# A folded Fourier projection: row-tile folds every third tile in a fixed order on two engines, and query swaps ahead of their sums

## The chip, the cores and the metric

One core of a Trainium2 chip runs the whole program in one launch. The engines are called as the profile calls them: PE (matrix multiply; PEld is its weight load), DVE (vector), ACT (scalar and activations), POOL (GpSimd), and SP, which only issues DMAs here. The metric is the device time of one execution in microseconds (us), less being better. Inputs and outputs are float32 and lie in device memory.

## The reference

Two layers of an encoder over 256 tokens and 16 learned tokens put in front (272 positions, width 2048). Cut to what matters here:

```python
h = rmsnorm(x, norm_mix[i])
proj = h @ w_in[i]                       # q | k | v | f | two gates
q, k, v = heads of proj                  # 8 query heads, 2 key/value heads, 128 wide
q = rope_2d(rmsnorm(q, q_norm[i])); k = rope_2d(rmsnorm(k, k_norm[i]))
attn = softmax(q k^T / sqrt(128)) v      # bidirectional
f = proj[..., OFF_F:OFF_GA]              # 8 groups of 128 channels
fr = fft2(f over (positions, channels of a group), norm="ortho").real
merged = sigmoid(ga) * (attn @ w_attn_br[i]) + sigmoid(gf) * (fr @ w_four[i])
x = x + merged @ w_out[i]
h2 = rmsnorm(x, norm_ffn[i])
x = x + (silu(dwconv3(h2 @ w_up_gate)) * (h2 @ w_up_val)) @ w_down[i]
```

After the second layer the 16 learned positions are dropped, so that layer computes queries and everything behind them for 258 columns, the 256 tokens and two neighbours for the convolution, while keys, values and the Fourier branch still see all 272.

## The kernel before

Activations lie transposed in on-chip memory: channels across the 128 partitions, positions along the free axis. Weights are read once, as a stream of chunks of 512 KB (128 partitions x 1024 float32; 512 contraction rows by 256 output columns). Each chunk passes through the same steps:

- SP issues its load into one of four `raw` buffers (line 179).
- ACT rounds it to the format that PE multiplies at full rate, giving the hi part `wh` (line 213); DVE subtracts that from the raw chunk, giving the lo part `wl` (line 214). Each has three buffers. The text calls these the hi split and the lo split. The lo split is the last reader of `raw`, so it releases that buffer for a later load.
- PE multiplies. A float32 product is made of three: hi weight by hi activation, hi weight by lo activation, lo weight by hi activation (lines 270, 271, 272 in `group`).

`advance(upto)` issues loads and puts splits on a list `todo`, two chunks ahead of the one that PE is at (`LOOK = 2`); `pump` takes the next split from the list, or all up to a chunk.

Besides the stream there are shadow generators: pieces of work (statistics of keys and queries, rotations, attention, folds) written as Python generators. `push(gen, wait)` adds one. After every second column product, `group` calls `step`, which counts each generator's wait down and runs the first one that is due up to its next `yield n`; n is the number of steps until it is due again. `until(hold, flag)` runs generators at once until a flag is set. So the yields set where in the written program the pieces of side work lie.

A scheduler then orders each engine's instructions from the written program and its own estimates. Within `tc.manual_schedule(engines={...})` the named engines keep the written order. Each engine executes its instructions strictly in order, and waits at an instruction until its inputs and buffers are ready.

The second layer (`last`, `lo = 14`) goes k, v, q0, q1, then the folded projection `f4`, then q2, q3 and the gates. A real 2-D transform over positions is even or odd under reflection, so the normalized activations are folded: for each row tile of 128 channels the sum and the difference of position t and its mirror position, 138 columns each, are multiplied with folded weights. The pieces, all of the second layer:

- `fold_pair(b)` (before) makes the folded row tiles 2b and 2b + 1. DVE multiplies by the norm (`t1`, line 645), adds (`hf`, 647); ACT copies two unpaired columns (648); DVE subtracts (649). Then, for each tile, ACT scales and rounds to the hi part (654), and DVE makes the lo part from it (655). There are eight slots, five in `hA` and three in `hB`.
- `fold_ahead` is a shadow generator that makes tiles 0 to 7 during earlier groups, from v on. `folded_f` makes tiles 8 to 15 while PE works on tiles 0 to 7, whose slots they take over.
- `folded_f` (line 663 on) runs over k = 0 to 15. One tile of work on PE is one weight chunk: four groups of channels by two halves, in eight banks, each with a hi product of hi and lo activations in one matmul (line 682) and a lo product (686). One pair of small matmuls for a separate column lies behind the first hi product of each tile (685). At k = 15 the groups are finished in the order 2, 3, 0, 1, and `E` is evacuated: ACT copies (689), DVE adds (690), ACT copies `e64` (692). Groups 2 and 3 lie in the same rotating set of banks ("mm") as the results of q0, q1, q2, so tile 0 needs q1's banks free, and q2 needs those of groups 2 and 3 free.
- `warm` (line 695) is a tiny Exp that loads ACT's table.
- `head_evac` takes a q or k group from its banks: per bank ACT squares (750) and DVE scales (751).
- `q_stage` and `kstats` are the generators behind q and k: `sums_t` transposes squares on PE (758) and reduces them on DVE (759); POOL raises to the power -1/2 (`pow_half`, 409); `swap` moves partition quarters by four DMAs (764) for the rotation; `rope` multiplies by sine and cosine (768 and 769), adds (770), rounds to hi on ACT (771), subtracts to lo on DVE (772). For keys, DVE spreads the factors along a mask (`dk`, 801), PE multiplies by ones to broadcast them (`ps_kb`, 804), and DVE applies them (805).

In this part of the kernel DVE keeps the written order from q1's evacuation through `folded_f`; ACT is ordered by the scheduler.

Of the kernel before, what the change touches and what calls it, by code (L numbers as in the profile page):

```python
# [20 lines left out]
T = NM + SEQ  # L21
# [107 lines left out]
def encoder_kernel(ctx, tc, xT, params, consts, bmat, cfold, csign, w_fl, w_f64c, w_in, w_abr, w_four, w_f64, w_out, w_up, w_down, outT):  # L129
# [77 lines left out]

    def split_w(i, a, b):
        if i not in splits:
            splits[i] = tuple(wp.tile([P, CW, MG * P], F32R, tag=t, name=f"{t}{i}") for t in ("wh", "wl"))  # L210
        h, lo = splits[i]
        r = raws[i]
        nc.scalar.copy(h[:, a:b], r[:, a:b])  # L213
        nc.vector.tensor_tensor(lo[:, a:b], r[:, a:b], h[:, a:b].bitcast(F32), op=ALU.subtract)  # L214
        if b == CW:
            del raws[i]

    shadow = []

    def push(gen, wait=0):  # L220
        shadow.append([wait, gen])
# [254 lines left out]
    for l in range(DEPTH):  # L476
# [6 lines left out]
        with tc.tile_pool(name=f"mix{l}", bufs=1) as mp:  # L483
# [158 lines left out]

            def fold_pair(b, slots):
                t1 = rt("t1")
                nc.vector.tensor_tensor(t1, XT[:, 2 * b:2 * b + 2, :], bc2(rstdB), op=ALU.mult)
                hf = rw("hf").rearrange("p k (e n) -> p k e n", e=2)
                nc.vector.tensor_tensor(hf[:, :, 0, 1:TH], t1[:, :, 1:TH], t1[:, :, T - 1:T - TH:-1], op=ALU.add)
                nc.scalar.copy(hf[:, :, 0, 0:T // 2 + 1:T // 2], t1[:, :, 0:T // 2 + 1:T // 2])
                nc.vector.tensor_tensor(hf[:, :, 1, :], t1[:, :, 1:TH + 1], t1[:, :, T - 1:T - TH - 1:-1], op=ALU.subtract)
                for q in range(2):  # L650
                    k = 2 * b + q
                    sl = slots[k % NS]
                    gc = prm[:, P_NM + l * KT + k:P_NM + l * KT + k + 1]
                    nc.scalar.activation(sl[:, :, 0, :], hf[:, q], AF.Copy, scale=gc)
                    nc.vector.scalar_tensor_tensor(sl[:, :, 1, :], hf[:, q], gc, sl[:, :, 0, :].bitcast(F32),
                                                   op0=ALU.mult, op1=ALU.subtract)

            def fold_ahead(slots):
                for b in range(NS // 2):
                    fold_pair(b, slots)  # L660
                    yield 2
                hold["ahead"] = True

            def folded_f(slots, E):
# [3 lines left out]
                for g in (0, 1, 2, 3):  # L668
                    ps[g] = [psum.tile([P, 512], F32, tag="aux" if g < 2 else "mm", name=f"ps_f{g}{e}") for e in range(2)]
                p64 = ps[0][0][:2 * NG, 2 * TH:3 * TH]  # L670
                for k in range(KT):
                    i = st["next"]
                    advance(i + 1 + LOOK)
                    pump(i)
                    h, lo_ = splits.pop(i)
                    st["next"] += 1
                    sl = slots[k % NS]
                    for g in ((2, 3, 0, 1) if k == KT - 1 else (0, 1, 2, 3)):
# [8 lines left out]
                        if k == KT - 1:  # L687
# [3 lines left out]
                            if g == 0:  # L691
                                nc.scalar.copy(e64, p64)
                        pump()
                    if k == 2:
                        nc.scalar.activation(warm, mhalf[:, 0:1], AF.Exp)
                    if k % 2 and k + NS < KT:
                        fold_pair((k + NS - 1) // 2, slots)

# [68 lines left out]
            def rope(hp, qs, H, L):  # L767
                tc.keep_in_program_order(nc.vector.tensor_tensor(qs, qs, bc2(sin), op=ALU.mult))
                tc.keep_in_program_order(nc.vector.tensor_tensor(hp, hp, bc2(cos), op=ALU.mult))
                nc.vector.tensor_tensor(hp, hp, qs, op=ALU.add)  # L770
                nc.scalar.copy(H, hp)
                nc.vector.tensor_tensor(L, hp, H.bitcast(F32), op=ALU.subtract)

# [15 lines left out]
            def kstats():  # L789
# [6 lines left out]
                pow_half(rk.rearrange("p a b -> p (a b)"), kss.rearrange("p a b -> p (a b)"))  # L796
                yield 4
                for kv in range(NKV):
# [9 lines left out]
                yield 8  # L808
                rope(kp, qs, kH, kL)
                hold["keys"] = True  # L810
# [42 lines left out]
            def q_stage(i, qp, qsq):  # L853
                kv, j = i // 2, i % 2
                sl = slice(2 * j, 2 * j + 2)
                if j == 0:
                    qvs.append(small.tile([P, 9], F32, tag="qv", name="qv"))
                    qsms.append(small.tile([P, 2, 4, NM], F32, tag="sqm", name="sqm", bufs=2))
                qv, qsm = qvs[kv], qsms[kv]
                nc.vector.tensor_copy(qsm[:, :, 2 * j:2 * j + 2, :], qsq[:, :, 0:NM].unsqueeze(1).to_broadcast([P, 2, 2, NM]))  # L860
                d4 = qv[:, 4 * j:4 * j + 4]
                sums_t(d4, [qsq[:, m, a:b] for m in range(MG) for a, b in BLK[1:]])
                d4 = d4.rearrange("p (m i) -> p m i", m=2)
                nc.vector.tensor_tensor(d4, d4, bc2(tok2[:, 1:3]), op=ALU.mult)
                qs = swap(qp)
                if j:
# [5 lines left out]
                    pow_half(rq, qv)  # L872
                yield 8 - j
                rope(qp, qs, qH[kv][:, sl, :], qL[kv][:, sl, :])
                if j:
# [111 lines left out]
            for i in range(4):  # L987
                ps = group((l, "q", i), xr(lo), W)
                if not (last and i == 1):
                    qq = head_evac(ps, prm[:, P_QN + l:P_QN + l + 1], "qp", lo)  # L990
                if last:
# [10 lines left out]
                if last and i == 1:  # L1002
                    until(hold, "ahead")
                    with tc.manual_schedule(engines={mybir.EngineType.DVE}):
                        qq = head_evac(ps, prm[:, P_QN + l:P_QN + l + 1], "qp", lo)
                        folded_f(slots, E)
                    o1_tiles()
                    push(folded_chan(E), 1)
                push(q_stage(i, *qq), 4)

# [183 lines left out]
```

## Time and profile before

| | us |
|---|---|
| Median of 3 runs | 2583.58 (2582.46 to 2586.19) |
| The profiled execution's own time | 2583.56 |
| Its span in the profile | 2581.7 |
| Mean granted clock of PE, share of full speed | 0.999 |

The profile page lists busy time per engine. A view of waits lists what an engine stood idle for: the instruction that waited, the one that released it, total, count, longest. A timeline has start, duration, engine, line, operation, `out<-in` by the program's names with the shapes, and a count where like instructions follow each other; the duration of such a row covers all of them. In brackets stands the idle time of that engine before the row, and its releaser. A view of windows has, for each stretch, the busy time of PE, PEld, DVE, ACT and POOL with instruction counts, PE's granted clock, the share of DMA engines busy and GB/s. DMA rows have a count, the size of one, and the median time from issue to landing. Matmuls overlap each other in the pipeline, so the starts of rows, not their durations, give PE's pace.

### The profile page before, as it was taken

Reading aid. Unit: us, or ns where it says so; the run is one execution under the profiler, and the core shown is the slowest. Engines: PE = TensorE matmul, PEld = TensorE weight load, DVE = VectorE, ACT = ScalarE, POOL = GpSimd, SP = SyncE. Lnnn points to the kernel's source line nnn. Section 1 sums busy time; section 2 is a strip of 40 time slices with the busy share of each in tenths; the row PEclk is TensorE's granted clock in tenths of the full one; section 3 lists DMA queues with packets and bytes.
Section 4 is the critical chain, followed back from the end, with each engine's and each line's share of the span. In section 5 each row is a group of like instructions: output and inputs, shape, how many; then the busy total and the mean of one; then the engine's idle time right before and its main releaser. Section 6 shows DMA issues by size and latency. Waiting matters only on the chain. (4 is left out here: it accounts for less than half of the span.)

```text
span 2581.7 us, 47873 instructions
## 1 busy us (share of the span) xinstructions
PE 2567.0 (99%) x19604; PEld 2502.1 (97%) x19604; DVE 1725.7 (67%) x2806; ACT 1215.9 (47%) x1763; POOL 19.6 (1%) x41
## 2 busy tenths in 40 slices
PE   9999999999999999999999999999999999999999
PEld 8999999999999999999999999999999998899988
DVE  7687766776666556666567877667766665566654
ACT  5455434554444334444444555345544543355443
POOL 0000000000000000000000000000000000000000
PEclk9999999999999999999999999999999999999999
DMA  6545555566766666666556446666555556555564
GB/s 234 162 154 164 189 182 185 183 204 226 230 226 229 223 227 223 226 220 213 172 164 208 148 152 198 191 191 194 181 187 187 183 187 188 187 187 185 185 199 159
DMA packets 142812, 499.21 MB, mean 193 GB/s; under 512 B 16368, under 2 KB 23152, under 8 KB 142592
## 3 DMA queue, kind: packets, MB, share of 16 engines
q1 hardware_dynamic: 140144, 494.02, 59.8%
q8 instruction: 153, 2.51, 0.4%
q10 hardware_dynamic: 2448, 2.13, 0.2%
q14 instruction: 67, 0.55, 0.1%
HBM read 474.43 MB, written 18.87 MB: 191 GB/s over the span
## 5 line engine op out<-in xcount | busy, mean ns | idle before, releaser
L214 DVE TENSOR_TENSOR wl<-raw,wh 128x1024 fp32r<-128x1024 f32 (+1 forms) x850 | 1037.1, 1222 | 712.6 <-ACT wh L213 708.3
L213 ACT CAST wh<-raw 128x1024 fp32r<-128x1024 f32 (+1 forms) x850 | 888.6, 1047 | 1064.0 <-issue 165.2
L271 PE MATMUL ps_ug<-xHL,wh 128*128 128x272 f32 (+1 forms) x1408 | 402.4, 286 | 0.0
L270 PE MATMUL ps_ug<-xHL,wh 128*128 128x272 f32 (+1 forms) x1408 | 402.0, 285 | 0.0
L272 PE MATMUL ps_ug<-xHL,wl 128*128 128x272 f32 (+1 forms) x1408 | 401.9, 285 | 0.0
L270 PEld LDWEIGHTS ps_ug<-xHL,wh 128*128 128x128 f32 x1408 | 265.4, 188 | 1.0
L271 PEld LDWEIGHTS ps_ug<-xHL,wh 128*128 128x128 f32 x1408 | 265.5, 189 | 0.1
L272 PEld LDWEIGHTS ps_ug<-xHL,wl 128*128 128x128 f32 x1408 | 264.9, 188 | 0.0
L266 PE MATMUL ps_uv<-xHL,wh 128*128 128x512 f32 x704 | 247.7, 395 | 0.0
L266 PE MATMUL ps_d<-gHL,wh 128*128 128x512 f32 x664 | 233.1, 395 | 0.0
L271 PE MATMUL ps_d<-gHL,wh 128*128 128x272 f32 (+1 forms) x744 | 214.4, 288 | 0.0
L270 PE MATMUL ps_d<-gHL,wh 128*128 128x272 f32 (+1 forms) x744 | 214.1, 288 | 0.0
L272 PE MATMUL ps_d<-gHL,wl 128*128 128x272 f32 (+1 forms) x744 | 214.0, 288 | 0.0
L271 PE MATMUL ps_uv<-xHL,wh 128*128 128x272 f32 x704 | 203.1, 288 | 0.0
L270 PE MATMUL ps_uv<-xHL,wh 128*128 128x272 f32 x704 | 202.9, 288 | 0.0
L272 PE MATMUL ps_uv<-xHL,wl 128*128 128x272 f32 x704 | 202.7, 288 | 0.0
L267 PE MATMUL ps_uv<-xHL,wl 128*128 128x256 f32 x704 | 197.7, 281 | 0.0
L267 PE MATMUL ps_d<-gHL,wl 128*128 128x256 f32 x664 | 186.6, 281 | 0.0
L266 PEld LDWEIGHTS ps_uv<-xHL,wh 128*128 128x128 f32 x704 | 132.4, 188 | 29.8
L266 PEld LDWEIGHTS ps_d<-gHL,wh 128*128 128x128 f32 x664 | 125.0, 188 | 29.2
L270 PE MATMUL ps_ga<-xHL,wh 128*128 128x272 f32 (+1 forms) x512 | 148.3, 290 | 0.0
L270 PE MATMUL ps_gf<-xHL,wh 128*128 128x272 f32 (+1 forms) x512 | 147.3, 288 | 0.0
(323 smaller groups left out, 5853.8 us busy)
## 6 DMA issues: line engine op xcount, KB each, us to landing
raw<-in_w_up SPq DMA_DIRECT2D x352, 512.0 KB, 3.5
raw<-in_w_in SPq DMA_DIRECT2D x191, 512.0 KB, 3.6
raw<-in_w_down SPq DMA_DIRECT2D x176, 512.0 KB, 3.5
raw<-in_w_out SPq DMA_DIRECT2D x64, 512.0 KB, 3.5
raw<-in_w_abr SPq DMA_DIRECT2D x32, 512.0 KB, 3.7
fw<-pfo SPq DMA_DIRECT2D x32, 512.0 KB, 4.7
raw<-fw SPq DMA_DIRECT2D x32, 512.0 KB, 4.3
raw<-in_w_four SPq DMA_DIRECT2D x16, 512.0 KB, 3.6
```

The source lines that it names most:

```text
L213: nc.scalar.copy(h[:, a:b], r[:, a:b])
L214: nc.vector.tensor_tensor(lo[:, a:b], r[:, a:b], h[:, a:b].bitcast(F32), op=ALU.subtract)
L266: nc.tensor.matmul(o2, h[:, c, sl], ab, start=kt == 0, stop=False)
L267: nc.tensor.matmul(o, lo[:, c, sl], ab[:, 0, :], start=False, stop=kt == nk - 1)
L270: nc.tensor.matmul(o, h[:, c, sl], a, start=kt == 0, stop=False)
L271: nc.tensor.matmul(o, h[:, c, sl], b, start=False, stop=False)
L272: nc.tensor.matmul(o, lo[:, c, sl], a, start=False, stop=kt == nk - 1)
```

## The change

- `fold_pair` becomes `fold_sum` (norm, add, subtract on DVE, then the column copy and the two scalings on ACT; the subtraction now comes ahead of the column copy) and `fold_low` (DVE's two lo parts). `fold_ahead` yields 2 between them, and 1 behind.
- In `folded_f` each iteration writes the hi split of the chunk two ahead first, then `fold_low` of a fold begun in the iteration before, then, at k = 2, 5, 8 and 11, the next `fold_sum`, and then the lo split. The tiles' pump calls go.
- DVE and ACT both keep the written order there; DVE's fixed order now begins with the group q1 itself.
- `warm` moves from k = 2 to k = 13.
- `rope` becomes a generator with a step between the hi rounding and the lo subtraction.
- `kstats` yields 6 instead of 4 ahead of `dk`. `q_stage` is pushed with a wait of 1 instead of 4; its swap DMAs come ahead of the sums, with a yield of 3 between, and the later yield is 6 - j instead of 8 - j.

What is multiplied by what stays the same. In the changed kernel lines from 214 to 645 lie 2 lower down, later ones between 2 and 20 lower.

```diff
 
-    def split_w(i, a, b):
+    def split_w(i, a, b, parts="hl"):
         if i not in splits:
...
         r = raws[i]
-        nc.scalar.copy(h[:, a:b], r[:, a:b])
-        nc.vector.tensor_tensor(lo[:, a:b], r[:, a:b], h[:, a:b].bitcast(F32), op=ALU.subtract)
-        if b == CW:
-            del raws[i]
+        if "h" in parts:
+            nc.scalar.copy(h[:, a:b], r[:, a:b])
+        if "l" in parts:
+            nc.vector.tensor_tensor(lo[:, a:b], r[:, a:b], h[:, a:b].bitcast(F32), op=ALU.subtract)
+            if b == CW:
+                del raws[i]
 
...
 
-            def fold_pair(b, slots):
+            def fold_sum(b, slots):
                 t1 = rt("t1")
...
                 nc.vector.tensor_tensor(hf[:, :, 0, 1:TH], t1[:, :, 1:TH], t1[:, :, T - 1:T - TH:-1], op=ALU.add)
+                nc.vector.tensor_tensor(hf[:, :, 1, :], t1[:, :, 1:TH + 1], t1[:, :, T - 1:T - TH - 1:-1], op=ALU.subtract)
                 nc.scalar.copy(hf[:, :, 0, 0:T // 2 + 1:T // 2], t1[:, :, 0:T // 2 + 1:T // 2])
-                nc.vector.tensor_tensor(hf[:, :, 1, :], t1[:, :, 1:TH + 1], t1[:, :, T - 1:T - TH - 1:-1], op=ALU.subtract)
+                for q in range(2):
+                    k = 2 * b + q
+                    nc.scalar.activation(slots[k % NS][:, :, 0, :], hf[:, q], AF.Copy, scale=prm[:, P_NM + l * KT + k:P_NM + l * KT + k + 1])
+                return hf
+
+            def fold_low(b, slots, hf):
                 for q in range(2):
...
                     sl = slots[k % NS]
-                    gc = prm[:, P_NM + l * KT + k:P_NM + l * KT + k + 1]
-                    nc.scalar.activation(sl[:, :, 0, :], hf[:, q], AF.Copy, scale=gc)
-                    nc.vector.scalar_tensor_tensor(sl[:, :, 1, :], hf[:, q], gc, sl[:, :, 0, :].bitcast(F32),
-                                                   op0=ALU.mult, op1=ALU.subtract)
+                    nc.vector.scalar_tensor_tensor(sl[:, :, 1, :], hf[:, q], prm[:, P_NM + l * KT + k:P_NM + l * KT + k + 1],
+                                                   sl[:, :, 0, :].bitcast(F32), op0=ALU.mult, op1=ALU.subtract)
 
...
                 for b in range(NS // 2):
-                    fold_pair(b, slots)
+                    hf = fold_sum(b, slots)
                     yield 2
+                    fold_low(b, slots, hf)
+                    yield 1
                 hold["ahead"] = True
...
                 p64 = ps[0][0][:2 * NG, 2 * TH:3 * TH]
+                hf = None
                 for k in range(KT):
...
                     advance(i + 1 + LOOK)
-                    pump(i)
+                    ahead = [j for j, _ in todo]
+                    todo.clear()
+                    for j in ahead:
+                        split_w(j, 0, CW, "h")
+                    if hf is not None:
+                        fold_low(hf[0], slots, hf[1])
+                        hf = None
+                    if k % 3 == 2 and k < 3 * (KT - NS) // 2:
+                        hf = NS // 2 + k // 3, fold_sum(NS // 2 + k // 3, slots)
+                    for j in ahead:
+                        split_w(j, 0, CW, "l")
+                    if k == 13:
+                        nc.scalar.activation(warm, mhalf[:, 0:1], AF.Exp)
                     h, lo_ = splits.pop(i)
...
                                 nc.scalar.copy(e64, p64)
-                        pump()
-                    if k == 2:
-                        nc.scalar.activation(warm, mhalf[:, 0:1], AF.Exp)
-                    if k % 2 and k + NS < KT:
-                        fold_pair((k + NS - 1) // 2, slots)
 
...
                 nc.scalar.copy(H, hp)
+                yield 1
                 nc.vector.tensor_tensor(L, hp, H.bitcast(F32), op=ALU.subtract)
...
                 pow_half(rk.rearrange("p a b -> p (a b)"), kss.rearrange("p a b -> p (a b)"))
-                yield 4
+                yield 6
                 for kv in range(NKV):
...
                 yield 8
-                rope(kp, qs, kH, kL)
+                yield from rope(kp, qs, kH, kL)
                 hold["keys"] = True
...
                 qv, qsm = qvs[kv], qsms[kv]
+                qs = swap(qp)
+                yield 3
                 nc.vector.tensor_copy(qsm[:, :, 2 * j:2 * j + 2, :], qsq[:, :, 0:NM].unsqueeze(1).to_broadcast([P, 2, 2, NM]))
...
                 nc.vector.tensor_tensor(d4, d4, bc2(tok2[:, 1:3]), op=ALU.mult)
-                qs = swap(qp)
                 if j:
...
                     pow_half(rq, qv)
-                yield 8 - j
-                rope(qp, qs, qH[kv][:, sl, :], qL[kv][:, sl, :])
+                yield 6 - j
+                yield from rope(qp, qs, qH[kv][:, sl, :], qL[kv][:, sl, :])
                 if j:
...
             for i in range(4):
-                ps = group((l, "q", i), xr(lo), W)
                 if not (last and i == 1):
+                    ps = group((l, "q", i), xr(lo), W)
                     qq = head_evac(ps, prm[:, P_QN + l:P_QN + l + 1], "qp", lo)
...
                     with tc.manual_schedule(engines={mybir.EngineType.DVE}):
-                        qq = head_evac(ps, prm[:, P_QN + l:P_QN + l + 1], "qp", lo)
-                        folded_f(slots, E)
+                        ps = group((l, "q", i), xr(lo), W)
+                        with tc.manual_schedule(engines={mybir.EngineType.Activation}):
+                            qq = head_evac(ps, prm[:, P_QN + l:P_QN + l + 1], "qp", lo)
+                            folded_f(slots, E)
                     o1_tiles()
                     push(folded_chan(E), 1)
-                push(q_stage(i, *qq), 4)
+                push(q_stage(i, *qq), 1)
 
```

## Prediction

> **What bounds the kernel now.** I read the page's busy shares first, then the waits of PE around the folded projection, then that stage instruction by instruction on PE, DVE and ACT.
>
> ```profile
> span 2581.7 us, 47873 instructions
> PE 2567.0 (99%) x19604; PEld 2502.1 (97%) x19604; DVE 1725.7 (67%) x2806; ACT 1215.9 (47%) x1763; POOL 19.6 (1%) x41
> ```
>
> PE is busy 2567.0 of 2581.7 us, so only 14.7 us of idle exists, plus whatever PE loses while counted as busy. The change leaves PE's matmuls as they are and shifts few of them; it can only win back stalls or make new ones. The stage that it rewrites is the folded projection of layer 1, 16 row tiles (k = 0 to 15), each on one 512 KB weight chunk. The waits of PE from 1380 to 1422 us (total, times, longest):
>
> ```profile
> PE ps_f L686 <- DVE wl L214: 3.8, 3, 1.6
> PE ps_f L682 <- DVE qp L751: 0.9, 1, 0.9
> PE ps_q L270 <- DVE E L690: 0.3, 1, 0.3
> ```
>
> Its PE timeline (start, duration; idle before in brackets). Each tile has one L685 pair, 0.13 us behind the tile's start, so these pairs are a clock for the tiles; L270 at the end is the first matmul of q2:
>
> ```profile
> 1380.32 0.29 PE L682 MATMUL ps_f<-hA,wh 128*128 128x276 f32 x1
> 1380.45 0.30 PE L685 MATMUL ps_f<-hA,w64s 128*16 128x138 f32 x2
> ...
> 1383.67 0.29 PE L685 MATMUL ps_f<-hA,w64s 128*16 128x138 f32 x2
> 1385.76 0.30 PE L685 MATMUL ps_f<-hA,w64s 128*16 128x138 f32 x2
> ...
> 1396.87 0.33 PE L686 MATMUL ps_f<-hB,wl 128*128 128x138 f32 x1 [1.57 <-DVE wl L214]
> ...
> 1402.83 0.34 PE L686 MATMUL ps_f<-hA,wl 128*128 128x138 f32 x1 [1.55 <-DVE wl L214]
> ...
> 1414.98 0.29 PE L685 MATMUL ps_f<-hB,w64s 128*16 128x138 f32 x2
> 1417.06 0.30 PE L685 MATMUL ps_f<-hB,w64s 128*16 128x138 f32 x2
> ...
> 1421.56 0.39 PE L270 MATMUL ps_q<-xHL,wh 128*128 128x258 f32 x1 [0.34 <-DVE E L690]
> ```
>
> Undisturbed, a tile takes 2.09 us (1383.67 to 1385.76; 2.08 from 1414.98 to 1417.06); I use 2.087. The stage takes 1421.56 - 1380.32 = 41.24 us against 16 x 2.087 = 33.4: 7.8 us are lost. The first tile accounts for 3.22 - 2.09 = 1.1, the three waits on lo splits for 3.8, and part of the rest is in the clock (columns: us, busy of PE, PEld, DVE, ACT, POOL, granted clock, DMA share, GB/s):
>
> ```profile
> 1403.00:1407.00 4.00, 4.00 (x22) 3.92 (x23) 2.68 (x5) 1.94 (x5) 0.00 (x0) 0.57 0.71 215
> 1407.00:1421.00 14.00, 14.00 (x121) 13.64 (x120) 8.90 (x9) 7.28 (x9) 0.25 (x2) 1.00 0.88 272
> ```
>
> Four us at 0.57 cost 4 x 0.43 = 1.7 us. What is left, about 1.2, is start-up behind each wait and the end of the stage.
>
> Why the lo splits are late shows on DVE, which runs here in program order, and on ACT:
>
> ```profile
> 1394.76 0.92 DVE L655 SCALAR_TENSOR_TENSOR hA<-hf,prm,hA 128x276 fp32r<-128x276 f32 x2 [1.29 <-ACT hA L654]
> 1395.60 2.35 DVE L214 TENSOR_TENSOR wl<-raw,wh 128x1024 fp32r<-128x1024 f32 x2
> 1397.87 0.72 DVE L645 TENSOR_TENSOR t<-XT,rstdB 128x544 f32<-128x544 f32 x1
> ...
> 1398.98 0.44 DVE L649 TENSOR_TENSOR hf<-t 128x276 f32<-128x276 f32 x1
> 1400.71 0.51 DVE L655 SCALAR_TENSOR_TENSOR hA<-hf,prm,hA 128x276 fp32r<-128x276 f32 x1 [1.29 <-ACT hA L654]
> ```
>
> ```profile
> 1399.10 0.20 ACT L648 COPY hf<-t 128x4 f32<-128x4 f32 x1 [3.02 <-DVE hf L647]
> 1399.20 1.04 ACT L213 CAST wh<-raw 128x1024 fp32r<-128x1024 f32 x1
> 1400.15 0.52 ACT L654 ACTIVATE hA<-hf,prm 128x276 fp32r<-128x276 f32 x1
> ```
>
> One round (a fold of two tiles and two lo splits) lasts 1400.71 - 1394.76 = 5.95 us, while PE needs 2 x 2.087 = 4.17 for the two tiles. In each, DVE stands 1.29 us idle at L655, because ACT puts a hi split of 1.04 between the small copy and the two activations. Four rounds, each 1.8 late, use up the lead of two chunks and then stop PE.
>
> **The change, part by part.** *Folds.* The instructions are the same; the rhythm is new: a fold every third tile, its sums (L645, L647, L649) in one iteration, its two L655 in the next, the hi split ahead of the fold on ACT, one lo split at the end of each iteration. DVE per three tiles: three lo splits of 1.15 (2.35 / 2, overlap counted) = 3.5, sums 1398.98 + 0.44 - 1397.87 = 1.55, lows 0.84 (1394.76 to 1395.60): 5.9 against 3 x 2.087 = 6.26. Neither DVE's total nor ACT's (3 x 1.04 + 0.2 + 0.9 = 4.2) exceeds it, and the wait at L655 falls away, since the activations are done before the next iteration. Worked from a tile's start S: hi split done S + 1.2, sums S + 1.9, lo split S + 3.05 in a fold iteration; S + 2.9 with lows ahead of it; S + 2.45 otherwise. The split is of chunk k + 2, wanted at S + 4.2: 1.1 to 1.7 us in hand. All three waits and the half-clock stretch go. Raw loads from 1380 to 1422 (count, size, median us from issue to landing):
>
> ```profile
> raw<-fw SPq DMA_DIRECT2D x11, 512.0 KB, 4.3
> raw<-in_w_in SPq DMA_DIRECT2D x5, 512.0 KB, 5.6
> ```
>
> ```profile
> DMA packets 2714, 8.64 MB, mean 206 GB/s; under 512 B 338, under 2 KB 722, under 8 KB 2710
> ```
>
> A buffer is released by the lo split of four chunks earlier, at S + 3.05 at worst, and its chunk is wanted 4 x 2.087 later, plus 0.13: 5.4 us for a landing that takes 4.3 (the row of 5.6 is from the burst after PE's stops). Tight, but I charge nothing; uncovered, it costs the lateness itself.
>
> (The last row is all traffic from 1380 to 1422; rival C needs it.)
>
> *The start.* The last evacuation of q1 frees the banks that tile 0 needs:
>
> ```profile
> 1380.37 0.48 DVE L751 SCALAR_TENSOR_TENSOR qp<-ps_q,prm,rstdB 128x258 f32<-128x258 f32 x1
> 1382.03 0.73 DVE L772 TENSOR_TENSOR q<-qp,q 128x544 fp32r<-128x544 f32 x1 [1.18 <-ACT q L771]
> 1382.67 0.48 DVE L751 SCALAR_TENSOR_TENSOR qp<-ps_q,prm,rstdB 128x258 f32<-128x258 f32 x1
> ```
>
> Before, the rotation's subtraction L772 waits 1.18 for ACT ahead of the second L751. The new order has the subtraction first, on a copy that ACT makes between q1's two squares and no longer behind a hi split: I put it at 1380.05 to 1380.8. Then come a lo split (1.15) and both L751 (0.4 each behind one another), to about 1382.7 instead of 1382.67 + 0.48 = 1383.15. The loss goes from 1.1 to 0.65.
>
> *The end.* The Exp table load, 1.28 us, moves from L918 to k = 13:
>
> ```profile
> L918 ACT ACT_TABLE_LOAD x1 | 1.3, 1283 | 0.0
> ```
>
> It was off the critical path and now delays one hi split, inside the lead. But E's adds, which release q2's banks, now stand behind a hi split (1.05) and a lo split (1.22) in fixed order: tile 15 starts, the splits end 2.43 later, the add 2.70 later. Before it was 1421.56 - (1417.06 - 0.13 + 2.09) = 2.54. Cost 0.15.
>
> Stage: 0.65 + 15 x 2.087 + 2.70 = 34.65, a gain of 41.24 - 34.65 = 6.6 us.
>
> *Key statistics.* kstats yields 6 instead of 4, so in layer 1's v group DVE's order changes, too:
>
> ```profile
> 1346.41 1.02 DVE L759 TENSOR_REDUCE kss<-ps_ss 128x3 f32<-128x384 f32 x2
> ...
> 1348.12 0.17 DVE L794 TENSOR_SCALAR kss<-kss 128x6 f32<-128x6 f32 x1
> 1348.19 1.23 DVE L214 TENSOR_TENSOR wl<-raw,wh 128x1024 fp32r<-128x1024 f32 x1
> ...
> 1350.79 0.24 DVE L801 TENSOR_SCALAR dk<-cst,rk 128x16 f32<-128x16 f32 x1
> ...
> 1351.64 0.49 DVE L801 TENSOR_SCALAR dk<-cst,rk 128x128 f32<-128x128 f32 x2
> ```
>
> ```profile
> 1338.11 0.86 POOL L409 TENSOR_TENSOR tok<-ms,mhalf 128x3 f32<-128x3 f32 x1 [7.25 <-DVE ms L458]
> ...
> 1348.37 2.23 POOL L409 TENSOR_TENSOR rk<-kss,mhalf 128x6 f32<-128x6 f32 x1 [9.41 <-DVE kss L794]
> ```
>
> ```profile
> 1351.94 0.29 PE L270 MATMUL ps_v<-xHL,wh 128*128 128x272 f32 x1
> 1352.28 0.70 PE L804 MATMUL ps_kb<-dk,ones 128*128 128x272 f32 x2
> ```
>
> In the changed order the lo split (1.23) comes ahead of the scaling L794, from about 1347.4, so L794 is at about 1348.6; POOL's power starts 0.25 behind it and takes between 0.86 (three columns) and 2.23 (six), so rk is ready 1349.7 to 1351.1. Behind the first dk (0.24) then stand two fold sums, two lows and a lo split (0.36 + 0.44 + 0.84 + 1.15) and the two dk of 0.49: dk is complete at 1353.3 to 1354.7. PE's matmul L804 comes nine matmuls later, 1352.07 + 9 x 0.125 = 1353.2 (1352.07 is the last L270 plus a step). So PE waits 0.1 to 1.5, against 1352.28 - 1352.07 = 0.2 before: net -0.1 to 1.3. I take 1.0, towards the end that this very operation showed. Behind L804 in PE's order stands all of v.
>
> [...]
>
> *The rest.* The rotation's yield, swaps ahead of the sums, shorter yields: the same instructions, in places where DVE is 67% and ACT 47% busy and PE works on splits made two chunks ahead. That cover is worth zero; without it I allow 0.5 either way, and charge 0.2 for the second kb product and the attention's shifted products.
>
> **Sum.** 6.6 - 1.0 - 0.2 = 5.4 us from the profiled execution's 2583.56, which is the median's 2583.58 as near as matters: **2578.2 us**. Own range 2576.4 to 2579.6.
>
> **The rivals.** *A: a half-clock stretch stays or comes anew, 1.7 us: 2579.9.* For: in before it followed waits of only 1.57 and 1.55, and a kb stall of 1.0 to 1.3 is not far from that. Against: it needed two within 6 us, and the lone wait of 0.9 on L751 was followed by none. [...]
>
> *B: the folds fit but a chunk lands late at the end, 2 to 3 us: about 2580.8.* The loads of cos/sin tables and q1's swap are queued on SP ahead of a raw chunk, and E's adds now stand behind its split. For: 5.6 above. Against: 5.4 us and only some 0.3 MB ahead of it.
>
> *C: the other side. The stream of weights is the bound of the stage.* Before, 206 GB/s went through in the stage; 16 chunks of 0.524 MB at that rate take 40.7 us, a gain of 0.5, less 1.0 at kb and 0.2: 2584.3, slower than before. It decides below 8.39 MB / (41.24 - 1.2) = 210 GB/s. The new pace wants 251. Against: 272 GB/s over 14 us in the row above.
>
> *D: the change doesn't do what it says.* L655 still waits for ACT or lo splits are late in every fold, the stage stays near 40: gain 1, less 1.2: 2583.8. It takes 0.4 us more DVE work per three tiles than I count to run out of cover at all.
>
> **Numbers.** Forecast 0.62, A 0.16, B 0.10, C 0.05, D 0.05, and 0.02 for what I haven't seen. A measurement of this kernel tells about 0.2% (5.2 us) from no change, so faster means below 2578.4, a hair above the forecast. Within its own range the kb stall can shrink by 1.1 and grow by 0.3, and the 0.2 may be nothing: some seven tenths of it lie below 2578.4, 0.43, and 0.01 of the unseen: faster 0.44. The rest of the forecast, A, B and D, and C at 2584.3 are within 0.2%: same 0.51. Slower 0.05 takes C or D together with A's clock and a wait that I haven't found. The range, 2575.9 to 2582.6, takes in A and B and the bounds of the unknown costs, and leaves out C, D and a tail below.
>
> **What would show it.** In the changed profile: L685 pairs 2.09 apart from k = 1 on, no PE wait on lo splits, clock 1.00 throughout, q2 beginning 34.7 us after the first folded matmul; a PE wait at the kb product on dk of about 1.2; POOL's power there at 0.86 to 2.23. Wrong if the pairs still spread, if the granted clock dips near the kb product, or if waits appear in layer 0's q groups.

## The result and the profile after

The changed kernel takes 2579.41 us (median of 22 runs, 2578.52 to 2582.61) against 2583.5 for the kernel before (22 runs beside them). The ratio is 0.9984, with a 95% interval of 0.9977 to 0.999: a gain of 4.1 us, 0.16%. The profiled execution of the changed kernel took 2579.72 us itself, with a span of 2577.9, 3.8 less than before.

The busy shares of the changed kernel's page, the waits of PE from 1382 to 1419 us, and its windows there (columns as before):

```profile
PE 2565.2 (100%) x19604; PEld 2500.5 (97%) x19604; DVE 1726.5 (67%) x2806; ACT 1215.4 (47%) x1763; POOL 19.7 (1%) x41
```

```profile
PE ps_q L272 <- DVE E L711: 0.5, 1, 0.5
PE ps_f L703 <- DVE qp L767: 0.3, 1, 0.3
```

```profile
1383.00:1419.00 36.00, 35.25 (x301) 34.33 (x300) 32.32 (x48) 25.02 (x41) 0.25 (x2) 1.00 0.75 249
```

No wait on a lo split is left in the folded stage, the granted clock is 1.00, and 249 GB/s go through where it was 206. PE's timeline shows the even beat:

```profile
1383.20 0.29 PE L703 MATMUL ps_f<-hA,wh 128*128 128x276 f32 x1
1383.33 0.30 PE L706 MATMUL ps_f<-hA,w64s 128*16 128x138 f32 x2
...
1386.08 0.29 PE L706 MATMUL ps_f<-hA,w64s 128*16 128x138 f32 x2
1388.15 0.29 PE L706 MATMUL ps_f<-hA,w64s 128*16 128x138 f32 x2
...
1400.69 0.29 PE L706 MATMUL ps_f<-hA,w64s 128*16 128x138 f32 x2
1402.78 0.29 PE L706 MATMUL ps_f<-hA,w64s 128*16 128x138 f32 x2
...
1417.84 0.38 PE L272 MATMUL ps_q<-xHL,wh 128*128 128x258 f32 x1 [0.46 <-DVE E L711]
```

From the first folded matmul to q2 it is 1417.84 - 1383.20 = 34.64 us, against 41.24. But the stage starts 2.88 us later than before, so something ahead of it has given time away. Where, is seen by setting the first matmul of each section against the same one before:

| Section begins | before | after | later by | lost or won since the row above |
|---|---|---|---|---|
| layer 0, keys | 61.49 | 62.36 | 0.87 | +0.87 |
| layer 0, a late gate group | 283.63 | 285.15 | 1.52 | +0.65 |
| layer 1, q0 | 1355.70 | 1359.07 | 3.37 | +1.85 |
| folded stage | 1380.32 | 1383.20 | 2.88 | -0.49 |
| layer 1, q2 | 1421.56 | 1417.84 | -3.72 | -6.60 |
| last matmul | 2578.02 | 2574.09 | -3.93 | -0.21 |

The first row isn't the change: up to layer 0's keys the program is the same but for one Exp of 0.2 us, and in the runs below, where that part is the same too, this number goes from -1.19 to +2.35; it is the loading at the start, which differs from run to run. (The three XT loads of 544 KB landed 7.7 us after their issue in the median, 6.4 before, and ACT's first four activations on them begin at 11.60, before at 10.64.) The third and fourth rows belong together, since the second key product has moved from q0 into v: 1.36 us. PE's wait there, and what DVE and POOL did:

```profile
1356.24 0.70 PE L821 MATMUL ps_kb<-dk,ones 128*128 128x272 f32 x2 [1.35 <-DVE dk L818]
```

```profile
1348.93 1.22 DVE L216 TENSOR_TENSOR wl<-raw,wh 128x1024 fp32r<-128x1024 f32 x1
1350.07 0.17 DVE L811 TENSOR_SCALAR kss<-kss 128x6 f32<-128x6 f32 x1
1350.14 0.45 DVE L649 TENSOR_TENSOR hf<-t 128x274 f32<-128x274 f32 x1
1350.49 0.45 DVE L650 TENSOR_TENSOR hf<-t 128x276 f32<-128x276 f32 x1
1350.85 0.72 DVE L647 TENSOR_TENSOR t<-XT,rstdB 128x544 f32<-128x544 f32 x1
1352.79 0.23 DVE L818 TENSOR_SCALAR dk<-cst,rk 128x16 f32<-128x16 f32 x1 [1.21 <-POOL rk L411]
...
1354.48 1.22 DVE L216 TENSOR_TENSOR wl<-raw,wh 128x1024 fp32r<-128x1024 f32 x1
1355.62 0.47 DVE L818 TENSOR_SCALAR dk<-cst,rk 128x128 f32<-128x128 f32 x2
```

```profile
86.16 1.33 POOL L411 TENSOR_TENSOR rk<-kss,mhalf 128x6 f32<-128x6 f32 x1 [16.81 <-DVE kss L811]
...
1350.32 2.44 POOL L411 TENSOR_TENSOR rk<-kss,mhalf 128x6 f32<-128x6 f32 x1 [9.84 <-DVE kss L811]
```

The lo split lies ahead of L811, as the prediction had it, the power takes 2.44, and the two wide dk come behind another lo split; they end at 1356.09, and PE's product follows 0.15 us later.

### The profile page after: what moved, and what is told of

It reads as the page before. It is cut to its first block, busy times and chain, and to the rows that moved or that the text cites. A ratio compares the mean times of both kernels' runs of the same rounds, so it can differ in the third digit from the quotient of the medians.

```text
span 2577.9 us, 47874 instructions
## 1 busy us (share of the span) xinstructions
PE 2565.2 (100%) x19604; PEld 2500.5 (97%) x19604; DVE 1726.5 (67%) x2806; ACT 1215.4 (47%) x1763; POOL 19.7 (1%) x41
## 4 chain that ended last, share of the span: by engine, by line
PE 98%; DMA 1%; issue 1%; DVE 0%; ACT 0%; POOL 0%; SPq 0%; DVEq 0%; POOLq 0%; ACTq 0%
PE ps_ug L273 7%; PE ps_ug L272 7%; PE ps_ug L274 7%; PE ps_uv L268 6%; PE ps_d L268 6%; PE ps_d L272 4%; PE ps_d L273 4%; PE ps_d L274 4%; PE ps_uv L272 3%; PE ps_uv L273 3%; PE ps_uv L274 3%; PE ps_uv L269 3%; PE ps_d L269 3%; PE ps_gf L272 2%; PE ps_gf L273 2%; PE ps_o L273 2%
```

## The experiments

Each is told by the sections of the table above, which one profile of each kernel gives to about 0.1 us, while whole times scatter by a few us. What varies from one execution to the next, such as the landing of a load, is not averaged in this.

**The fold part alone.** The key statistics, rotation and query stages are those of before; the rest is the change.

```diff
-                yield 1          # rope
...
-                yield 6          # kstats
+                yield 4
...
-                yield from rope(kp, qs, kH, kL)
+                rope(kp, qs, kH, kL)
...
-                qs = swap(qp)
-                yield 3
...
+                qs = swap(qp)
...
-                yield 6 - j
-                yield from rope(qp, qs, qH[kv][:, sl, :], qL[kv][:, sl, :])
+                yield 8 - j
+                rope(qp, qs, qH[kv][:, sl, :], qL[kv][:, sl, :])
...
-                push(q_stage(i, *qq), 1)
+                push(q_stage(i, *qq), 4)
```

> Only the fold part of the change (sums and lows split, every third tile, DVE and ACT in written order, Exp at k = 13); rotation, key statistics and query stages as before. Theory: the whole 6.6 us come from the fold part, and the losses elsewhere from the new yields: the folded stage takes 34.6 to 35.1 us from its first matmul to q2, PE waits at most 0.5 us at the key product, layer 0 loses nothing, and the time is 1 to 2 us below the changed kernel's (about 2578). Rival: the earlier query swaps and rotations are needed for the stage; then it takes more than 37 us.

Measured: 2578.67 us (median of 10; ratio to before 0.9985, 0.9976 to 0.9994). That is 0.7 below the changed kernel's median where 1 to 2 were expected, and against the kernel before, run beside each, both gain 4.1: no difference is shown. The profiled execution took 2585.8, the longest of the ten; half clock behind its gap at q2 for 10.2 us (last section) and once at the start for 3.4 us makes 6.8 of the 7.1 us by which it lies above the median, so it is read up to q2 only.

Layer 0 loses nothing between the keys and the late gate group (0.65 in the changed kernel); so that loss comes from the new yields and swaps. The other runs bear this out: 0.65 to 0.71 in the six that keep them, -0.03 to 0.01 in those that don't. Kstats at 4 alone keeps it, so the rotations and query stages make it; which of their yields and swaps is open. The tiles run evenly, without a wait on lo splits. But the wait at the key product is still there, 1.0 us in two pieces, against the expectation of at most 0.5, and the profiled stage took 37.59 us, not 34.6 to 35.1. By the number that is the rival's outcome, but of the 2.95 more than in the changed kernel 2.2 are at E's add and 0.7 in tile 0, and the mended kernel below takes 33.48 with the old swaps, so the earlier ones aren't needed. Its waits of PE:

```profile
PE ps_q L272 <- DVE E L711: 2.7, 1, 2.7
PE ps_f L703 <- DVE qp L767: 1.0, 1, 1.0
PE ps_kb L820 <- DVE dk L817: 1.0, 2, 0.8
```

The first row is q2's first matmul waiting for E's add. What E's add waited for, on ACT and DVE:

```profile
1413.31 1.03 ACT L214 CAST wh<-raw 128x1024 fp32r<-128x1024 f32 x1
1417.22 1.04 ACT L214 CAST wh<-raw 128x1024 fp32r<-128x1024 f32 x1 [2.88 <-PE ps_f L707]
1418.17 1.15 ACT L710 COPY E<-ps_f 128x138 f32<-128x138 f32 x6
```

```profile
1418.30 1.22 DVE L216 TENSOR_TENSOR wl<-raw,wh 128x1024 fp32r<-128x1024 f32 x1 [2.70 <-ACT wh L214]
1419.44 1.33 DVE L711 TENSOR_TENSOR E<-ps_f,E 128x138 f32<-128x138 f32 x6
```

The hi split ahead of E's copies begins 2.88 us late. The view names PE, whose matmul L707 had long been done; what is left is the raw chunk, whose load SP issued at 1409.50 and which landed 7.6 us later, at 1417.1. In three other runs the view names it; one of them:

```profile
1415.98 1.05 ACT L214 CAST wh<-raw 128x1024 fp32r<-128x1024 f32 x1 [1.40 <-DMA raw<-in_w_in]
```

**kstats at 4 in the changed kernel** (that row of ACT is from this run).

```diff
-                yield 6          # kstats
+                yield 4
```

> The changed kernel with kstats yielding 4 again. Theory: the 1.35 us that PE waits at the key product come from the yield of 6, which lets two folds' work and a lo split in ahead of dk; with 4 the wait is at most 0.5 us, the folded stage stays at 34.6, and the time is about 1.3 us below the changed kernel's. Rival: POOL's power (2.4 us) and its late start set that wait whatever follows; then 1.0 us or more stays.

Measured: 2580.17 us (ratio 0.999, 0.998 to 1.0), 0.8 above the changed kernel's median where 1.3 below was expected. The wait at the key product is 1.0 us, 0.8 and 0.2: the expectation failed, and the yield isn't the main cause. L811, which feeds the power, stands behind the lo split as in the changed kernel:

```profile
1348.04 1.22 DVE L216 TENSOR_TENSOR wl<-raw,wh 128x1024 fp32r<-128x1024 f32 x1
1349.17 0.17 DVE L811 TENSOR_SCALAR kss<-kss 128x6 f32<-128x6 f32 x1
```

The stage took 36.42, not 34.6, with 1.3 lost at q1's banks and 1.2 at E's add.

**A fold every second tile; sums and lows at once; both.** Three kernels; the third on top of the mended one below.

```diff
-                    if k % 3 == 2 and k < 3 * (KT - NS) // 2:
-                        hf = NS // 2 + k // 3, fold_sum(NS // 2 + k // 3, slots)
+                    if k % 2 == 0 and 0 < k <= KT - NS:
+                        hf = NS // 2 + k // 2 - 1, fold_sum(NS // 2 + k // 2 - 1, slots)
```

> The changed kernel with a fold at k = 2, 4, 6, 8 (its lows in the next iteration) instead of every third. Theory: DVE's work per round decides: 2.3 + 1.55 + 0.84 = 4.7 us against 4.17 on PE, so four rounds run 2.2 late, less 1.2 in hand: PE waits about 1.0 us in all on lo splits and the stage takes about 35.7 us. Rival: only the wait for ACT at the low parts mattered; then the stage stays at 34.6 with no wait on lo splits.

```diff
-                        hf = NS // 2 + k // 3, fold_sum(NS // 2 + k // 3, slots)
+                        fold_low(NS // 2 + k // 3, slots, fold_sum(NS // 2 + k // 3, slots))
```

> The changed kernel with the low parts right behind the sums in the same iteration, every third tile as it is. Theory: DVE waits about 0.9 us for ACT's two activations in each fold, a round of three tiles is 6.8 us against 6.26, four rounds run 2.1 late, less 1.1 in hand: PE waits 0.3 to 1.0 us on lo splits, the stage takes 35.0 to 35.7 us. Rival one: the rhythm alone did it; 34.6. Rival two: splitting sums and lows is the whole of it; 38 us or more.

> The mended kernel with the rhythm of before: a fold at k = 2, 4, 6, 8, sums and lows at once; only the place of the hi split (ahead of the fold on ACT) differs from before. Theory: a DVE round is then 2.3 + 1.55 + 0.65 + 0.84 = 5.35 us against 4.17, 1.2 late in each; three rounds make 3.5, less 1.3 in hand: PE waits 1.5 to 2.5 us on lo splits, in two or three pieces of at most 1.2, without a drop of the clock, and the stage takes 35 to 36.5 us. Rival: the hi split's place is the whole cause; then at most 0.3 us of such waits.

Measured. Every second tile: no wait on lo splits at all; DVE's rounds last 4.70 us as counted (1393.24, 1397.93, 1402.64), but four rounds have only three intervals between them: 3 x 0.53 = 1.6 late against some 1.3 in hand, and that is nearly hidden: one tile shows 0.2 us more than 2.09. My count of rounds was wrong; the outcome by itself is also what the rival had, and only the third kernel, whose longer rounds bring the waits back, speaks for the mechanism. (The stage's 35.99 us come from 1.1 at E's add and 1.1 in tile 0.)

Lows at once: rounds of 6.45 us, DVE 0.66 idle in each; four tiles show 0.2 us more than 2.09, 0.8 in all, inside what was expected. (Its stage took 36.63, above the 35.0 to 35.7 expected, because PE also waited 1.4 at E's add and 0.6 at q1's banks.)

Both together give DVE rounds of 5.32 us and waits again:

```profile
1393.71 0.33 PE L714 MATMUL ps_f<-hB,wl 128*128 128x138 f32 x1 [0.94 <-DVE wl L216]
1399.04 0.33 PE L714 MATMUL ps_f<-hA,wl 128*128 128x138 f32 x1 [0.92 <-DVE wl L216]
1404.36 0.33 PE L714 MATMUL ps_f<-hA,wl 128*128 128x138 f32 x1 [0.92 <-DVE wl L216]
```

2.8 us of them, a stage of 37.20 (a little more than expected). This kernel differs in its folds from before mainly in where the hi split stands on ACT: with that, DVE's wait at the lows goes from 1.29 to 0.66 and a round from 5.95 to 5.32, and 1 us of waits and the drop of the clock are gone. Beside it, either of the other two measures nearly ends the waits; the change has both. A kernel with these two and the hi split in its old place was not tried.

**E's evacuation first.** One move in the changed kernel: at k = 15 the split of q2's second chunk is written behind the evacuation of groups 2 and 3.

```diff
+                    held = ahead if k == KT - 1 else []
                     for j in ahead:
-                        split_w(j, 0, CW, "h")
+                        if j not in held:
+                            split_w(j, 0, CW, "h")
...
                             if g == 0:
                                 nc.scalar.copy(e64, p64)
+                            if g == 3:
+                                for j in held:
+                                    split_w(j, 0, CW)
```

> The changed kernel with one move: at k = 15 the split of the chunk after next (raw chunk 2 of q2) comes behind E's evacuation of groups 2 and 3 on ACT and DVE, not ahead of it. Theory: q2 waits for E's adds because they stand behind that split, and the split waits for a raw load whose landing varies (PE waited 0.5, 1.2, 1.1, 1.4 and 2.7 us there in five runs). With the move the wait is 0 to 0.2 us whenever the load lands, the stage loses 0.5 to 1 us against the changed kernel, and the time is 0.5 to 1.5 us lower. Rival: the evacuation itself is late; then 0.4 us or more stays.

Measured: 2578.45 us (11 runs, 2578.08 to 2579.46; ratio 0.9981, 0.9972 to 0.999), 1.0 below the changed kernel's median (the kernel before, run beside each, differs by 0.2). PE has no wait at q2, and the stage takes 34.02 us. No run lies above 2579.5, where the changed kernel reached 2582.6 in twice as many. So the evacuation itself isn't late; the split ahead of it was.

**The lo split behind q1's evacuations**, on top of that.

```diff
-                    pump()
+                    if key == (1, "q", 1) and j == len(chs) - 1:
+                        if todo:
+                            late.append(todo.pop(0)[0])
+                            split_w(late[-1], 0, CW, "h")
+                    else:
+                        pump()
...
-                    for j in ahead:
+                    for j in late + ahead:
```

> As the run before, and the lo split that lies ahead of q1's two evacuations on DVE goes behind them (its hi split stays). Theory: the wait of PE on q1's banks (0.3 to 1.3 us in five runs) comes from that split; it goes to 0 to 0.2 us, and tile 1 begins 2.1 to 2.3 us behind tile 0. Rival: the rotation's subtraction ahead of them, which hangs on the swap DMAs, is what is late; then 0.3 us or more stays.

Measured: no gain (2578.81, one run). PE waits 0.2 at q1's banks, as the theory had it, but then 0.4 for the lo split that was moved: tile 1 begins 2.63 us behind tile 0, and the stage takes 34.48. What was saved at one place is paid at the next, and the rival was right in that the rotation ahead is late. On DVE in this run its sine product waits for the swap's DMA:

```profile
1380.23 0.72 DVE L796 TENSOR_TENSOR qs<-qs,cst 128x544 f32<-128x544 f32 x1 [1.22 <-DMA qs<-qp]
```

**The key power's input.** In the changed kernel and, apart from it, in the kernel before:

```diff
# the changed kernel, fold_ahead whole
-                    hf = fold_sum(b, slots)
+                    fold_low(b, slots, fold_sum(b, slots))
                     yield 2
-                    fold_low(b, slots, hf)
-                    yield 1
# the kernel before, kstats at 6
-                yield 4
+                yield 6
```

> The changed kernel with fold_ahead making sums and lows in one go, and nothing else; kstats still yields 6. Theory (the split of fold_ahead alone lets a lo split go ahead of the key power's input): PE waits at most 0.3 us at the key product. Rival (both are needed: the yield of 6 puts dk behind more work): 0.7 us or more.

> The kernel before with kstats yielding 6 instead of 4 and nothing else. Theory: with fold_ahead in one go the powers' input stays ahead of the lo split, but dk comes behind another split and sums: PE waits 0.5 to 1.5 us at the key product. Rival: the yield alone costs nothing (PE's product moves back by as much as dk does): at most 0.3 us; then the split of fold_ahead is the whole cause.

Measured: PE has no wait at the key product in either. In the first, the power's input (L809 here) stands ahead of the lo split again; in the second, too:

```profile
1351.18 0.17 DVE L809 TENSOR_SCALAR kss<-kss 128x6 f32<-128x6 f32 x1
1351.25 1.23 DVE L216 TENSOR_TENSOR wl<-raw,wh 128x1024 fp32r<-128x1024 f32 x1
```

The yield of 6 costs nothing there without the split of fold_ahead (the product and its dk move behind v together), and with the split, 4 left 1.0 us. So the two-part fold_ahead is the cause: with it the scheduler puts a lo split ahead of L811. The first of these kernels loses again what it won: 2.5 us of waiting at E's add, and 1.5 more at the start of the execution than the changed kernel's profile (2581.91, one run). The second took 2585.99 (one run): its stage is 43.87 long, with two drops of the clock where the kernel before has one (last section).

**All mended**: the fold part alone, with both moves and fold_ahead whole.

> The fold part alone (as in the run with the fold part only) with both moves of the runs before, and fold_ahead making sums and lows in one go as before the change. Theory: the wait at the key product (1.35 us in the changed kernel, 0.8 with kstats at 4) comes from fold_ahead's split, which moves the powers' input behind a lo split; now it is 0 to 0.4 us, layer 0 gives back 0.6 us, q2 and q1's banks cost nothing: 2 to 3 us below the changed kernel, about 2576.5 to 2577.5. Rival: POOL's power keeps PE waiting at the key product whatever the order; then 0.7 us or more stays there.

Measured: 2575.69 us (6 runs, 2574.79 to 2575.94; ratio to before 0.997, 0.9958 to 0.9981), 3.7 below the changed kernel and a little more than the 2 to 3 expected. All waits of PE in its whole profile:

```profile
PE ps_f L345 <- ACT wh L214: 5.4, 3, 4.5
PE ps_nb L475 <- DVE tok L478: 0.7, 1, 0.7
PE ps_f L347 <- DVE wl L216: 0.5, 1, 0.5
```

All three lie at the start, in code that is the same in every kernel. The stage takes 33.48 us, 0.1 above 16 x 2.087. Here the lo split behind q1's evacuations costs nothing, because the swap isn't late. SP issued the swap 9 us ahead of the first folded matmul here and in the changed kernel. But it issued the three raw loads ahead of the swap from 15.3 us before that matmul on here (1365.09), and from only 13.5 on in the changed kernel (1369.70). The swap's parts landed in 3.0 us (median) here, in 4.3 in the changed kernel, and in 5.3 in the kernel with the lo split moved, where DVE waited. The changed kernel with nothing but fold_ahead made whole has 15.3 and 3.0 as well. So the split of fold_ahead, and with it the wait at the key product, is what crowds the raw loads up to the swap; that it does so by holding up lo splits is the likely way, and was not tried by itself.

**Gaps put in on purpose.** In the mended kernel at k = 4 lo splits are repeated, which changes no result.

```diff
+                            for x in range({4: 3}.get(k, 0)):      # the second kernel: {4: 4}
+                                nc.vector.tensor_tensor(splits[j][1], raws[j], splits[j][0].bitcast(F32), op=ALU.subtract)
                             split_w(j, 0, CW, "l")
```

> The mended kernel with three lo splits repeated at k = 4 (DVE works 3.4 us more, the results are the same): PE stands about 1.6 us once, and 0.5 us a tile later. Theory A (the kernel before: a wait of 1.57 passed once without a drop, and led to one another time): the clock may stay; the stage is about 2.2 us longer, or 3.9 with a drop. [...]

> The mended kernel with four lo splits repeated at k = 4: PE stands about 2.7 us once. Theory A (the run with the fold part only had one gap of 2.67 us and then half clock for 8.9 us): the clock drops to 0.5 for 3.4 us or more, and the stage is 5 to 8 us longer than the mended one. [...]

Measured: a gap of 1.65 us left the clock at 1.00; the stage grew by 2.4 to 35.87. A gap of 2.91 was followed by a drop, and the stage grew by 4.7 to 38.19, of which 1.7 is the clock. The gap and the window behind it, of the second kernel:

```profile
1397.68 0.33 PE L716 MATMUL ps_f<-hB,wl 128*128 128x138 f32 x1 [2.91 <-DVE wl L216]
```

```profile
1398.00:1402.00 4.00, 4.00 (x24) 3.92 (x22) 3.93 (x7) 3.01 (x5) 0.00 (x0) 0.57 0.55 187
```

So the clock can drop behind a single gap of 2.91 us, as theory A had it, though the growth of 4.7 was a little under its 5.

## Why the prediction was right, and where it was off

- *The folds: right.* Rounds, times in hand and the even beat came as worked out; the changed stage took 34.64 us where 34.65 was forecast. Which part of the change does it is a finding of the experiments: the hi split's place alone doesn't, with either of the other two it nearly does; whether it is needed was not tried. (A slip of reading: at k = 15 the L685 pair lies about 1.0 us further behind the tile's start, for the order of groups 2, 3, 0, 1; the sums used tile 14's pair and stand.)
- *The start: right in that execution, and luck in part.* Tile 0 took 2.75 instead of 3.22, as the 0.45 had it; in five other kernels with this code at q1's end it took from 2.74 to 3.77. The rotation ahead of the evacuations hangs on a swap whose landing varies (3.0, 4.3 and 5.3 us in the median of its parts in three kernels).
- *The end: mis-sized.* "The add 2.70 later", a cost of 0.15, held in the profiled execution (2.66 from tile 15's start to q2), and that was luck. I took q2's second raw chunk as landed by then. In six profiles with this order (the changed kernel, and the kernels with the fold part only, kstats at 4, every second tile, lows at once and fold_ahead whole) PE waited 0.5, 2.7, 1.2, 1.1, 1.4 and 2.5 us there: 1.6 in the mean, where the forecast's 0.15 makes 0.5. The load of that chunk landed 5.2 us after its issue in the changed kernel and 6.1, 7.6 and 7.4 in those with kstats at 4, the fold part only and fold_ahead whole, with the same transfers on SP ahead of it; what makes it vary isn't shown. Rival B had the place and the queue; it is a part of the forecast's own case, not another one.
- *The key product: right in its order, undersized.* The wait was 1.35, net 1.15 by the wait and 1.36 by the sections, for the 1.0 taken. The cause was put down to the yield of 6 and is the split of fold_ahead, which was in the same diff; the yield goes with 0.35 of it (1.35 against 1.0).
- *The POOL power: above the range that was taken.* The prediction had 0.86 to 2.23, and two sums of DVE behind the first dk. Two sums and the next norm product ran beside the power (1350.14 to 1351.57), and it took 2.44. In layer 0, with DVE idle beside it (for 1.44 us), the same shape took 1.33, in the kernel before as well, so 0.86, measured on three columns, was too low a bound for it. With kstats at 4 and 0.6 us of DVE's work beside it, it took 1.80, and in the kernel before, with such work beside the whole of it, 2.23. The times with DVE at work beside it are the longer ones, but 2.23 stood beside more of it than 2.44; that DVE's work is what lengthens the power was not tried by itself.
- *The rest: mis-sized.* 0.2 was charged, layer 0 alone lost 0.65, and an allowance of 0.5 didn't hold it. Of these 0.4 is a wait of PE on the attention's value products (L975). Without the new yields and swaps it is gone, and the whole 0.65 with it.
- *Rivals.* A: no drop in the changed kernel's profile, so the gain of 1.7 was kept there. But the three slowest of its 22 runs (2581.44, 2582.2, 2582.61) have a mean granted clock of 0.999 and the others 1.000; one drop of 3.4 us takes 0.0007 of the span, so A probably came true in these. "It needed two within 6 us" is refuted: lone gaps of 2.67 (E's add, the fold part only) and 2.91 were enough, and in the kernel with the yield of 6 the drop came at the first gap of 1.57. C: 249 GB/s, so the stream isn't the bound. D: the beat says no.

The sum by sections: -6.60 + 1.36 + 0.65 - 0.21 = -4.80, and +0.87 from the start of that execution makes -3.93. The forecast's 5.4 was 1.3 too much against the measured 4.1, and 2579.41 lies just inside its own range. The sections account for 0.6 of it (5.4 against 4.80); in the median the rest is E's add, whose move won 1.0, and the start of the execution, not separated here.

## What to carry to other kernels

A side job beside a stream has to fit its period on each in-order engine, waits on the other engine included (before, a round of 5.95 us on DVE against PE's 4.17 stopped PE three times): write the two engines' rounds down, and give the job a round of three tiles where it doesn't fit in two. But a fixed order also fixes who waits behind whom: work that releases banks must not stand behind a split that hangs on a load, even where the load "should" be there (PE waited 0.5 to 2.7 us there in the six profiles with that order). After such a change, compare the start of every section with before: what was won in one place was here paid back in two others, and the best kernel is the one that left those alone.

## What the runs showed of the hardware

The clock's drop was not a matter of the gap's length alone. In the kernel before, a gap of 1.57 us left it at 1.00 and the next, of 1.55, did not; the same stage in the kernel with only the yield of 6 changed dropped at both, the second time for longer. That kernel's gaps, and the slices of 0.2 us in which its clock changes:

```profile
1396.73 0.33 PE L686 MATMUL ps_f<-hB,wl 128*128 128x138 f32 x1 [1.57 <-DVE wl L214]
...
1408.62 0.44 PE L686 MATMUL ps_f<-hA,wl 128*128 128x138 f32 x1 [1.56 <-DVE wl L214]
```

```profile
1398.40:1398.60 0.20, 0.20 (x4) 0.20 (x3) 0.17 (x2) 0.00 (x0) 0.00 (x0) 0.64 0.92 369
1401.80:1402.00 0.20, 0.20 (x4) 0.20 (x3) 0.20 (x1) 0.08 (x1) 0.00 (x0) 0.83 0.00 0
1408.60:1408.80 0.20, 0.18 (x1) 0.18 (x2) 0.20 (x1) 0.17 (x1) 0.00 (x0) 0.74 0.69 171
1415.40:1415.60 0.20, 0.20 (x3) 0.20 (x2) 0.00 (x0) 0.00 (x0) 0.00 (x0) 0.70 1.38 246
```

The clock between such changes reads 0.50 (the kernel before, 1403.20 to 1406.20), so the share in such a slice tells where in it the change lay: half clock from 1398.46 to 1401.87 and from 1408.70 to 1415.52. That is 3.41 and 6.82 us, and the second starts 10.24 us after the first: one, two and three times 3.41. So in this execution the drops began and ended on a fixed beat, and not at the gaps, which ended at 1396.73 and 1408.62. The gap of 2.91 was followed by 3.4 us, like the one of the kernel before, and the gap of 2.67 by three times that, 1419.03 to 1429.27:

```profile
1419.00:1419.20 0.20, 0.00 (x0) 0.00 (x0) 0.20 (x1) 0.20 (x3) 0.00 (x0) 0.57 0.75 307
1429.20:1429.40 0.20, 0.20 (x3) 0.20 (x2) 0.20 (x1) 0.00 (x0) 0.00 (x0) 0.83 0.00 0
```

Gaps of 1.65 and 2.49 were followed by none.

A gap's place on the beat fits what it did, if the beat is taken to run on ahead of the first drop, which is an estimate of mine from the 3.41. In the kernel before half clock lasted from 1403.02 to 1406.44 (the slices at its ends read 0.56 and 0.91); counted back from its start by 3.41, the gap that dropped it (1401.28 to 1402.83) lies within one interval, and the one that did not (1395.30 to 1396.87) is cut in two at 1396.20. Both gaps of the other kernel lie within one. That is four gaps, and they show no rule; why two drops lasted two and three intervals stays open.

The rounded format's rate on PE shows at the keys' product, whose tiles are plain float32 (L804, 272 columns, in the kernel before). From its start at 87.96 to 88.55 pass it and one rounded product of 272 columns, 0.59 us; two rounded ones take 0.25.
